# Sample attention: the matmuls of a four-page unit as one group on TensorE, and the next transposition directly behind the weighted sum

## The chip, the core and the metric

The kernel runs on one core of one Trainium2 chip. The metric is the device time of one launch in microseconds (us). The kernel before was timed three times: 3252.61, 3260.63 and 3261.89 us, median 3260.63 us. One further execution was recorded by the hardware profiler, and every duration below is from that record.

The engines in the tables are PE (TensorE, matmuls), PEld (TensorE's weight loads), DVE (VectorE), ACT (ScalarE), POOL (GpSimd) and SP (SyncE, which here only issues DMAs). Each engine works through its own instructions strictly in program order.

## What is computed

One inference step of a hybrid layer for a prompt of 2048 tokens and, with the same weights, for 8 sample tokens that each attend over 16384 cached positions. For the samples the attention works on the cached latents directly. Cut to what matters here:

```python
q_lat   = einsum('bthd,rhd->bthr', q_nope, w_uk)                  # 8 samples, 8 heads, 256 latent dims
s_past  = einsum('bthr,bkr->bhtk', q_lat, c_past) + einsum('bthd,bkd->bhtk', q_rope, kr_past)
p       = softmax(concat([s_past, s_new]) * SCALE)
o_lat   = einsum('bhtk,bkr->bthr', p[..., :P], c_past) + ...      # P = 16384 = 128 pages of 128
o       = einsum('bthr,rhd->bthd', o_lat, w_uv)
# around it, for the prompt: gated MLP, causal attention, output projection, then
up = h @ w_up;  c = causal conv of width 3 over up;  y = (silu(c_gate) * c_val) @ w_down
```

`c_past` and `kr_past` are gathered through a page table: every sample has 128 pages, scattered over a pool.

## The kernel before

**The main work.** The prompt sets the order: input projections (up to about 330 us of the profile), gated MLP (to 570), causal attention (to 1130), output projection (to 1368), and then the feed-forward part in three token blocks of 688, 688 and 680 columns. A block runs through 22 feature steps. A feature step has four quarters, Q0 to Q3 (gate and value, each in two halves of the columns). Each quarter is 24 up-projection matmuls (`up`, 8 groups of 3) whose result DVE takes out of PSUM (`U`, L1727). Behind the matmuls of Q1, Q2 and Q3 stand 5, 5 and 6 pieces of the down-projection of the step before (`dp`, 3 matmuls each, three PSUM buffers), and DVE adds each piece to the output in SBUF (`y`, L1580), in program order. Behind the pieces of Q1 and Q3 follows the convolution: ACT forms `c` from `U` (L1556), DVE adds the two other taps (two SCALAR_TENSOR_TENSOR, L1557 and L1558). The weights are split into a high and a low part ahead of use: ACT writes the high part (`wdh` behind the pieces of Q1, `wu` behind those of Q2 and of Q3), POOL the low part (`wdl`, `wu`, L124).

**The sample attention** is a second stream of work, written as a generator (`sample_stream`). After every main matmul group the helper `fill(ns)` takes the nominal time of the group off a counter; when the counter is down to zero the next piece of the stream is issued, and its `yield` value is added to the counter. So a `yield` says how much main work goes on all engines' queues before the next piece. `st["per"]` sets the pace: 27000, 24000, 28000 and 20500 ns of main work for eight pages in the four stages; a unit of four pages has half of it.

The 8 samples are handled as two sets (s = 0, 1) of four samples, and each set in two phases of 32 units. Four tiles, one for each sample, hold the four pages of a unit.

- *Scores* (first half of the generator): 36 matmuls into one PSUM tile `sc`, nine rounds (`m`) of four samples. A sample uses 32 columns of the array, so that the four matmuls of a round sit in four column strips. Each fp32 matmul stands as two records in the profile, so that a unit has 72. Between rounds 2 and 3, and between 5 and 6, stands `yield 1400`. Then DVE takes the scores out of PSUM together with a running maximum (`S`, L705), the four tiles are given back, and `pump()` issues the DMAs for the tiles that came free on SP's queue. The pool has six tiles: two of the next unit are already on their way when a unit runs, and the other two can be fetched only when it is done.
- *Weighted sum* (second half): 16 matmuls into `po` with the transposed probabilities `pT` (8 columns of the array for each sample). `pT` of the next unit is made by `turned`: a transposition on TensorE (`pp`, L767) of a 128x128 part of `S`, and a copy out of PSUM on ACT (`pT`, L85). It stands 3000 ns of main work behind the sum.

The set s = 0 is scored during gated MLP and attention (336 to 925 us) and summed during the end of the attention, the output projection and the first feature steps (1001 to about 1550). The set s = 1 is scored in feature steps 7 of the first block to 1 of the second (1577 to 2055) and summed in steps 4 to 19 of the second block (2133 to 2600).

Of the kernel before, what the change touches and what calls it, by code (L numbers as in the profile page):

```python
# [28 lines left out]
NPG = 128  # L29
# [21 lines left out]
def build(tc, A):  # L51
# [17 lines left out]
    def mkpool(stack, name, bufs, space=None):  # L69
        kw = {} if space is None else {"space": space}  # L70
        return stack.enter_context(tc.tile_pool(name=name, bufs=bufs, reuse_waits="tile", **kw))


    def mm(out, w, x, start, stop):
        pe.matmul(out, lhsT=w, rhs=x, start=start, stop=stop)  # L75
# [8 lines left out]
    def copy(out, in_):  # L84
        act.activation(out, in_, AF.Copy)  # L85
# [505 lines left out]
    st = {"wait": 0.0, "done": False, "pool": mkpool(smp, "s_pg", SL), "slots": SL, "per": PA}  # L591

    def sample_stream():
# [9 lines left out]
        def slot(shape, name):  # L603
            return st["pool"].tile(shape, F32, tag="pg", bufs=st["slots"], name=name)
# [13 lines left out]
        def load_wuv(t):  # L618
            gq.dma_start(out=t, in_=A["w_uv"].rearrange("(k p) n -> p k n", p=128))
            return t  # L620

        def load_wx():
            k = 8 - left.pop()
            wx.append(slot([128, 1024], "wos"))
            gq.dma_start(out=wx[-1], in_=A["w_out"][k * 128:(k + 1) * 128, :])
# [3 lines left out]
        def pump():  # L629
            while held["n"] < st["slots"]:  # L630
                if not pending:
                    u = plan()
                    if u is None:
                        return
                    queue.append((u, []))
                    pending.extend((u, queue[-1][1], b) for b in range(4))
                (s, kind, p0, n), got, b = pending.pop(0)
                held["n"] += 1
                bb = 4 * s + b
                _, vs = nc.values_load_multi_w_load_instructions(  # L640
                    pt[bb:bb + 1, p0:p0 + n], engines=[SPE], min_val=0, max_val=NPOOL - 1,
                    skip_runtime_bounds_check_because="the table is clamped to the pool on the chip")
                if kind == 0:
                    t = slot([128, n, 288], "ct")
                    for j in range(n):
                        sp.dma_start(out=t[:, j, :], in_=A["cT"][bass.ds(vs[j], 1), :, :].rearrange("a p f -> p (a f)"))
                else:
                    t = slot([128, n // 4, 1024], "cn")
                    for j in range(n):
                        sp.dma_start(out=t[32 * (j % 4):32 * (j % 4) + 32, j // 4, :],  # L650
                                     in_=A["cN"][bass.ds(vs[j], 1), :, :].rearrange("a p f -> p (a f)"))
                got.append(t)

        def units(s, kind):
            done = 0
            while done < NPG:
                pump()
                if not queue:
                    yield None
                    continue  # L660
                (s_, kind_, p0, n), cts = queue.pop(0)
                assert (s_, kind_) == (s, kind) and len(cts) == 4
                done += n
                yield p0, n, cts
# [14 lines left out]
        for s in range(2):  # L679
# [6 lines left out]
            for unit in units(s, 0):  # L686
                if unit is None:
                    yield None
                    continue
                p0, n, cts = unit  # L690
                N = n * 32
                ps = sps.tile([128, 512], F32, tag="sc", name="sc")
                for m in range(9):
                    for b in range(4):
                        bb = 4 * s + b
                        o = ps[32 * b:32 * b + 32, 0:N]
                        if m < 8:
                            a, q = m // 4, m % 4
                            mm(o, qz[:, b, a, q, :], cts[b][:, :, a * 128 + 32 * q:a * 128 + 32 * q + 32], m == 0, False)
                        else:  # L700
                            mm(o, qrb[:, bb, :], cts[b][:, :, 256:288], False, True)
                    if m in (2, 5):
                        yield 1400
                j += 1
                dve.tensor_scalar(out=S[:, p0 * 32:p0 * 32 + N], in0=ps[:, 0:N], scalar1=1.0, scalar2=tops[:, j - 1:j] if j else NEG,  # L705
                                  op0=ALU.mult, op1=ALU.max, accum_out=tops[:, j:j + 1])
                held["n"] -= 4
                pump()
                yield st["per"] * n / 8 - 2800
            cnew = sc_p.tile([1, 4 * KVR], F32, tag="cnew", bufs=1, name="cnew")  # L710
            gq.dma_start(out=cnew, in_=A["o_slat"][4 * s:4 * s + 4, :].rearrange("(a b) k -> a (b k)", a=1))
            ps = sps.tile([128, 512], F32, tag="sc", name="scn")
# [52 lines left out]
            def turned(p0):  # L765
                pp = sps.tile([128, 512], F32, tag="sc", name="pp")
                pe.transpose(pp[:, 0:128], S[:, p0 * 32:p0 * 32 + 128], ident)  # L767
                pT = sc_p.tile([128, 128], F32, tag="pT", name="pT")
                copy(pT, pp[:, 0:128])
                return pT  # L770

            pT = turned(0)
            yield 3000
            for unit in units(s, 1):
                if unit is None:
                    yield None
                    continue
                p0, n, cns = unit
                if s == 1 and p0 + n == NPG:
                    wuv = load_wuv(slot([128, 2, 512], "wuv"))  # L780
                    load_wx()
                for q in range(4):
                    for b in range(4):
                        mm(po[32 * b:32 * b + 8, 0:256], pT[:, 32 * b + 8 * q:32 * b + 8 * q + 8],
                           cns[b][:, 0, q * 256:(q + 1) * 256], False, p0 + 4 == NPG and q == 3)
                held["n"] -= 4
                pump()
                yield 3000
                if p0 + 4 < NPG:
                    pT = turned(p0 + 4)  # L790
                yield st["per"] / 2 - 3000
            if s == 1:
                for _ in range(4):
                    load_wx()
# [62 lines left out]
        aq.dma_start(out=x2_sp[:, SEQ:TOK].rearrange("(k p) t -> p k t", p=128), in_=a)  # L857

    stream = sample_stream()

    def step():
# [1069 lines left out]
```

## Time and profile before

| | |
|---|---|
| three runs | 3252.61, 3260.63, 3261.89 us |
| profiled execution, first to last instruction | 3243.1 us (the profile gives no other time of this execution; the runs are 9.5 to 18.8 us above it) |
| PE busy | 3071.8 us, 95% |
| DVE, ACT, POOL busy | 63%, 37%, 34% |
| mean granted TensorE clock | 0.982 of full speed |
| DMA queues | q1 (SP's) 359.85 MB, q0 (POOL's) 196.59 MB |

The page lists, for each group of instructions, the busy time, the mean of one, and the idle time of the engine just before them with what ended it. PE is the engine to watch. A matmul is pipelined: its record is longer than the distance to the next one, so costs on PE are read from start to start, not from the records' lengths. The view by line merges both rounds and stages; the view of waits can be cut to a stretch of time, which tells the stages apart.

### The profile page before, as it was taken

To read this page: it belongs to the slowest core of one execution; us is meant where nothing else is said; L and a number is where in the kernel's file an instruction comes from. 1 tells how busy PE (TensorE), PEld (TensorE's weight loads), DVE (VectorE), ACT (ScalarE), POOL (GpSimd) and SP (SyncE) were. 2 spreads that over 40 slices of the span, in tenths; PEclk is the share of its full clock that TensorE was granted. 3 is DMA by queue.
4 is the path that set the end of the run, shared out by engine and by line. 5 is a ranking of instruction groups with operands and counts; after the bars stand their busy time and mean duration, and the time that the engine had idled before them with its cause. 6 is when DMAs were issued, how large, how long until landed. Compare 5 with 4: busy or idle time off the path is not lost. (4 is left out here: it accounts for less than half of the span.)

```text
span 3243.1 us, 66014 instructions
## 1 busy us (share of the span) xinstructions
PE 3071.8 (95%) x23958; PEld 2712.4 (84%) x23958; DVE 2038.9 (63%) x3670; ACT 1193.1 (37%) x2472; POOL 1098.3 (34%) x1102
## 2 busy tenths in 40 slices
PE   7999999999999999999999999999998998999997
PEld 7898777777777788889988898889887878989987
DVE  6555332676777744445666666766566668777777
ACT  5334332676787722232222223422222233322223
POOL 4332222422233244433332234433222334333332
PEclk9999999899999999999999999999999999999999
DMA  5446667777766789987566777658766634221222
GB/s 171 131 156 225 194 194 199 202 207 199 208 162 155 198 246 251 250 238 218 179 213 206 215 218 225 200 146 216 205 190 182 188 126 143 66 72 59 66 72 53
DMA packets 340434, 571.22 MB, mean 176 GB/s; under 512 B 59343, under 2 KB 247406, under 8 KB 340110
## 3 DMA queue, kind: packets, MB, share of 16 engines
q1 hardware_dynamic: 264128, 359.85, 38.6%
q0 software_dynamic: 56176, 196.59, 20.8%
q10 hardware_dynamic: 19806, 10.55, 1.1%
q8 instruction: 192, 3.15, 0.4%
q14 instruction: 132, 1.08, 0.1%
HBM read 504.62 MB, written 62.18 MB: 175 GB/s over the span
## 5 line engine op out<-in xcount | busy, mean ns | idle before, releaser
L75 PE MATMUL up<-h,wu 128*128 128x344 f32 (+2 forms) x6336 | 1068.9, 324 | 9.5 <-DVE U L1727 4.1
L75 PEld LDWEIGHTS up<-h,wu 128*128 128x128 f32 x6336 | 1002.2, 190 | 48.7 <-issue 29.8
L1580 DVE TENSOR_TENSOR y<-y,dp 128x344 f32<-128x344 f32 (+1 forms) x960 | 456.8, 510 | 49.4 <-PE dp L75 40.1
L124 POOL TENSOR_TENSOR wu<-wraw,wu 128x1024 fp32r<-128x1024 f32 x132 | 317.9, 2409 | 363.0 <-ACT wu L85 186.8
L124 POOL TENSOR_TENSOR wdl<-wraw,wdh 128x1024 fp32r<-128x1024 f32 x66 | 158.1, 2395 | 722.8 <-ACT U L1555 683.0
L75 PE MATMUL dp<-gh,wdh 128*128 128x344 f32 (+1 forms) x960 | 323.4, 337 | 78.7 <-DVE y L1580 78.6
L1556 ACT ACTIVATE c<-U,gn 128x688 f32<-128x688 f32 (+3 forms) x138 | 128.9, 934 | 653.1 <-DVE U L1727 653.1
L1727 DVE TENSOR_TENSOR U<-up,R 128x344 f32<-128x344 f32 (+2 forms) x264 | 134.5, 511 | 351.2 <-PE up L75 344.5
L75 PE MATMUL dp<-gl,wdh 128*128 128x344 f32 (+1 forms) x960 | 310.0, 323 | 0.0
L75 PE MATMUL dp<-gh,wdl 128*128 128x344 f32 (+1 forms) x960 | 309.4, 322 | 0.0
L75 PEld LDWEIGHTS dp<-gh,wdh 128*128 128x128 f32 x960 | 182.0, 190 | 106.6 <-DVE y L1580 94.4
L75 PE MATMUL s<-k,q 96*128 96x512 f32 (+2 forms) x960 | 259.0, 381 | 4.4 <-DVE mx L1201 2.1
L1557 DVE SCALAR_TENSOR_TENSOR c<-U,gn,c 128x688 f32<-128x688 f32 (+3 forms) x138 | 214.7, 1556 | 33.4 <-ACT c L1556 33.3
L124 DVE TENSOR_TENSOR pl<-t,ph 128x512 fp32r<-128x512 f32 (+1 forms) x320 | 194.2, 607 | 63.7 <-ACT ph L85 60.7
L1558 DVE SCALAR_TENSOR_TENSOR c<-U,gn,c 128x688 f32<-128x688 f32 (+3 forms) x138 | 223.7, 1621 | 4.9
L85 ACT ACTIVATE ph<-t 128x512 fp32r<-128x512 f32 (+1 forms) x320 | 170.1, 532 | 138.2 <-PE t L1223 134.2
L1211 ACT ACTIVATE S<-S,nm 128x512 f32<-128x512 f32 (+2 forms) x320 | 208.0, 650 | 6.8 <-POOL nm L1203 6.8
L75 PEld LDWEIGHTS s<-k,q 96*128 96x128 f32 x960 | 169.7, 193 | 46.7 <-issue 9.4
L75 PEld LDWEIGHTS dp<-gl,wdh 128*128 128x128 f32 x960 | 183.2, 191 | 1.2
L75 PEld LDWEIGHTS dp<-gh,wdl 128*128 128x128 f32 x960 | 182.6, 190 | 0.9
L1223 PE MATMUL t<-cst,S 128*128 128x128 f32 x1088 | 174.9, 275 | 2.4 <-DVE pl L124 2.1
L75 PE MATMUL sc<-ct,qz 128*32 128x128 f32 x4096 | 157.5, 279 | 13.1 <-DMA ct<-in_cT 13.1
(377 smaller groups left out, 5094.7 us busy)
## 6 DMA issues: line engine op xcount, KB each, us to landing
ct<-in_cT SPq DMA_DIRECT2D x1024, 144.0 KB
cn<-in_cN SPq DMA_DIRECT2D x1024, 128.0 KB
wraw<-in_w_up POOLq DMA_DIRECT2D x132, 512.0 KB, 4.1
wraw<-in_w_down POOLq DMA_DIRECT2D x66, 512.0 KB, 4.5
q_sp<-qs SPq DMA_DIRECT2D x48, 256.0 KB
xt<-in_xT SPq DMA_DIRECT2D x16, 512.0 KB
kn_sp<-qs SPq DMA_DIRECT2D x32, 256.0 KB
v_sp<-v SPq DMA_DIRECT2D x16, 512.0 KB
```

What stands on the lines that cost most here:

```text
L75: pe.matmul(out, lhsT=w, rhs=x, start=start, stop=stop)
L85: act.activation(out, in_, AF.Copy)
L124: (lo_eng or dve).tensor_sub(lo, src, f(hi))
L1211: act.activation(s, s, AF.Exp, scale=SCALE, bias=d["nm"][:, qb:qb + 1], accum_out=d["ls"][:, qb, r:r + 1])
L1223: pe.transpose(p[:, (qb - q0) * 128:(qb - q0) * 128 + 128], d["S"][qb, kb // 4][:, ks], ident)
L1556: act.activation(c[:, lo:hi], u[:, 2 + lo:2 + hi], AF.Identity, scale=w[2], bias=g(B_CONV, ix))
L1557: dve.scalar_tensor_tensor(out=c[:, lo:hp], in0=u[:, 1 + lo:1 + hp], scalar=w[1], in1=c[:, lo:hp], op0=ALU.mult, op1=ALU.add)
L1558: dve.scalar_tensor_tensor(out=c[:, lo:hp], in0=u[:, lo:hp], scalar=w[0], in1=c[:, lo:hp], op0=ALU.mult, op1=ALU.add)
L1580: dve.tensor_add(y, y, p[:, 0:nn])
L1727: dve.tensor_mul(u[:, 2 + o:2 + o + m], p[:, 0:m], RT[b][:, o:o + m])
```

## The change

The two inner `yield 1400` of the scores go, and the `yield` behind a unit grows by the same 2800 ns. The transposition for the next unit moves from 3000 ns of main work behind the weighted sum to directly behind it, ahead of the return of the tiles. The numbers of matmuls, transpositions, copies and DMAs stay the same, and so does the distance from the start of one unit to the start of the next in main work.

```diff
                             mm(o, qrb[:, bb, :], cts[b][:, :, 256:288], False, True)
-                    if m in (2, 5):
-                        yield 1400
                 j += 1
                 dve.tensor_scalar(out=S[:, p0 * 32:p0 * 32 + N], ...)
                 held["n"] -= 4
                 pump()
-                yield st["per"] * n / 8 - 2800
+                yield st["per"] * n / 8
...
+                if p0 + 4 < NPG:
+                    pT = turned(p0 + 4)
                 held["n"] -= 4
                 pump()
-                yield 3000
-                if p0 + 4 < NPG:
-                    pT = turned(p0 + 4)
-                yield st["per"] / 2 - 3000
+                yield st["per"] / 2
```

The order of PE's instructions at three places, the rows before with a minus and the changed ones with a plus. First, a unit of scores in the feed-forward part, in step 9 of the first block, among the pieces `dp` of Q2. `x12` is a group of 12 matmuls (24 records), `qrb` the last round.

```order
 L75 MATMUL dp<-gl,wdh 128x344
 L75 MATMUL dp<-gh,wdl 128x344
-L75 MATMUL sc<-ct,qz 32x128 x12
+L75 MATMUL sc<-ct,qz 32x128 x32
+L75 MATMUL sc<-ct,qrb 32x128 x4
 L75 MATMUL dp<-gh,wdh 128x344
 L75 MATMUL dp<-gl,wdh 128x344
```

All 36 now stand where the first 12 stood; the second and third group leave their places further on, in the `up` matmuls of Q3. All 64 units are changed in this way. DVE's `S` comes directly behind the group, so that it too stands earlier: here behind the second `y` of Q2.

Second, the weighted sum of s = 0 in step 2 of the first block: `po` stands among the five pieces of Q1, `pp` stood in the `up` matmuls of Q2.

```order
 L75 MATMUL dp<-gh,wdl 128x344
 L75 MATMUL po<-cn,pT 8x256 x16
+L765 MATMUL pp<-cst,S 128x128
 L75 MATMUL dp<-gh,wdh 128x344
 L75 MATMUL dp<-gl,wdh 128x344
...
 L75 MATMUL up<-h_5_18550,wu 128x344
-L767 MATMUL pp<-cst,S 128x128
 L75 MATMUL up<-h_6_18554,wu 128x344
 L75 MATMUL up<-h_6_18555,wu 128x344
```

The transposition moves from the `up` matmuls of Q2 in among the pieces of Q1 or right behind them. This is so in steps 1 to 5 of the first block. On ACT its copy `pT` comes ahead of `wdh` and of `c` of Q1 both before and now.

Third, the weighted sum of s = 1 in step 11 of the second block: `po` stands in the `up` matmuls of Q1, `pp` stood behind the five pieces of Q1.

```order
 L75 MATMUL po<-cn,pT 8x256 x16
+L765 MATMUL pp<-cst,S 128x128
 L75 MATMUL up<-h_6_27338,wu 128x344
 L75 MATMUL up<-h_6_27339,wu 128x344
...
 L75 MATMUL dp<-gl,wdh 128x344
 L75 MATMUL dp<-gh,wdl 128x344
-L767 MATMUL pp<-cst,S 128x128
 L75 MATMUL up<-h_0_27094,wu 128x344
 L75 MATMUL up<-h_0_27095,wu 128x344
```

Here the transposition moves out of the neighbourhood of the pieces, up into the `up` matmuls of Q1. In steps 11 to 19 of the second block it stood behind three, four or all five pieces of Q1; in steps 4 to 10 it stood in the `up` matmuls of Q2 and now goes into the `up` matmuls of Q1 or right behind them (in step 4 behind the first piece). The second transposition of each step, which stands in Q3, stays in Q3.

## The prediction

> **What bounds the kernel now.** I read the page first, then the waits of TensorE cut by stage, then the order of time around single units. The page:
>
> ```profile
> span 3243.1 us, 66014 instructions
> PE 3071.8 (95%) x23958; PEld 2712.4 (84%) x23958; DVE 2038.9 (63%) x3670; ACT 1193.1 (37%) x2472; POOL 1098.3 (34%) x1102
> ...
> L75 PE MATMUL sc<-ct,qz 128*32 128x128 f32 x4096 | 157.5, 279 | 13.1 <-DMA ct<-in_cT 13.1
> ```
>
> TensorE is busy for 95% of the span. 4096 records in 157.5 us of busy time are 38 ns each: four column strips overlap. The stretches in which the units run, by busy time of each engine (PE, PEld, DVE, ACT, POOL), then the granted clock, DMA share and GB/s:
>
> ```profile
> 575.00:925.00 350.00, 340.40 (x3062) 269.21 (x3062) 251.83 (x672) 237.64 (x608) 97.51 (x212) 0.98 0.77 206
> 1583.00:2055.00 472.00, 450.54 (x4464) 406.78 (x4463) 311.42 (x480) 123.05 (x207) 157.77 (x117) 1.00 0.71 216
> 2133.00:2600.00 467.00, 440.26 (x3338) 393.60 (x3338) 283.55 (x408) 109.98 (x205) 146.20 (x102) 0.97 0.70 195
> ```
>
> These are scoring in attention, scoring in the feed-forward part, and the weighted sum of s = 1. What TensorE waits for: first in 575 to 925, then in 1583 to 2055 (two rows), then in 2133 to 2600:
>
> ```profile
> PE sc L75 <- DMA ct<-in_cT: 6.4, 5, 3.1
> ...
> PE dp L75 <- DVE y L1580: 13.5, 12, 1.6
> PE sc L75 <- DMA ct<-in_cT: 6.7, 4, 3.9
> ...
> PE dp L75 <- DVE y L1580: 26.7, 9, 3.4
> ```
>
> In attention TensorE hardly waits for DVE or ACT, so time saved on TensorE there is time of the span. In the feed-forward part it waits for `y`: a fourth piece `dp` needs the buffer that DVE's first `y` frees. These waits have causes that the change moves, so they are terms of the sum.
>
> **Term 1, entries and exits of TensorE.** One unit of scores in the gated MLP, TensorE alone:
>
> ```profile
> 476.65 0.40 PE L75 MATMUL pu<-wa,hl 128*128 128x512 f32 x1
> 476.98 0.86 PE L75 MATMUL sc<-ct,qz 128*32 128x128 f32 x24
> 477.77 0.73 PE L75 MATMUL pu<-wa,hh 128*128 128x512 f32 x2
> 478.34 0.40 PE L75 MATMUL pu<-wa,hl 128*128 128x512 f32 x1
> 478.57 0.63 PE L75 MATMUL pu<-wa,hh 128*128 128x512 f32 x2
> 479.04 0.40 PE L75 MATMUL pu<-wa,hl 128*128 128x512 f32 x1
> ...
> 481.76 0.64 PE L75 MATMUL sc<-ct,qz 128*32 128x128 f32 x16
> 482.22 0.40 PE L75 MATMUL sc<-ct,qrb 128*32 128x128 f32 x8
> 482.55 0.73 PE L75 MATMUL pu<-wa,hh 128*128 128x512 f32 x2
> ...
> 477.33 0.51 PE L75 MATMUL sc<-ct,qz 128*32 128x128 f32 x12
> ```
>
> From `pu hl` to `pu hl` with a group between: 478.34 - 476.65 = 1.69 us; without: 479.04 - 478.34 = 0.70. A visit of 24 records costs 0.99 us. Inside, 16 records take 482.22 - 481.76 = 0.46 us, and 12 (the first 12 of the row that starts at 476.98, up to 477.33) take 0.35: four more records cost 0.11. Six such rounds are 0.66, so 0.33 us of each visit is neither matmul nor main work. A unit has three visits and keeps one: 2 x 0.33 x 64 units = 42 us. The bound below: if only the stretch from the first `sc` to the next `pu` (0.79 us) were shared, 0.79 - 0.66 = 0.13 is saved, 17 us in all. I take 42, since entry, exit and the late second `pu` are each tied to a change between the two kinds of matmul, and two of three changes go.
>
> The transposition gets no price. Its 64 instances occupy little, and whether one costs more or less behind `po` than alone this trace does not show:
>
> ```profile
> L767 PE MATMUL pp<-cst,S 128*128 128x128 f32 x64 | 17.5, 273 | 0.0
> ```
>
> Both ends lie within a fraction of 17.5 us; I take 0 with 4 either way.
>
> **Term 2, waits for pages.** The tiles are given back behind the first 36 matmuls instead of 2800 ns of main work later, and the next unit starts as far from this one as before. So a page has 2.8 us more. The waits are 6.4 + 6.7 = 13.1 us; the two longest (3.1, 3.9) would leave 0.3 and 1.1: 12 us saved. Below: 5, if SP's queue is itself late. POOL's queue issues as before.
>
> **Term 3, waits for `y` while scoring.** One step (DVE, ACT, POOL and TensorE mixed), with no transposition in it:
>
> ```profile
> 1628.02 0.52 DVE L1727 TENSOR_TENSOR U<-up,R 128x344 f32<-128x344 f32 x1 [0.67 <-PE up L75]
> ...
> 1630.72 2.39 POOL L124 TENSOR_TENSOR wu<-wraw,wu 128x1024 fp32r<-128x1024 f32 x1 [4.81 <-ACT wu L85]
> 1630.83 3.02 DVE L1557 SCALAR_TENSOR_TENSOR c<-U,gn,c 128x688 f32<-128x688 f32 x1
> ...
> 1633.88 3.24 DVE L1558 SCALAR_TENSOR_TENSOR c<-U,gn,c 128x688 f32<-128x688 f32 x1
> 1633.98 2.40 POOL L124 TENSOR_TENSOR wu<-wraw,wu 128x1024 fp32r<-128x1024 f32 x1
> ...
> 1637.47 2.32 DVE L1580 TENSOR_TENSOR y<-y,dp 128x344 f32<-128x344 f32 x5
> 1638.02 0.43 PE L75 MATMUL dp<-gh,wdh 128*128 128x344 f32 x1 [1.49 <-DVE y L1580]
> ```
>
> Both DVE passes of the convolution run beside a pass of POOL and take 3.0 and 3.2 us, and `y` comes late. TensorE waited 1.49 us although one visit (0.99) stood ahead of the fourth piece: uncovered it would be 2.5. In steps 8 to 20 the whole group now stands ahead of the fourth piece, with 0.33 + 18 x 0.11 = 2.3 us of cover, 1.3 more. Most of the 13.5 us goes. In half of the steps the group stands ahead of the first piece, and DVE takes `S` before `y`, which hands back some 0.4. I take 9 saved, ends 0 and 13.
>
> **Term 4, the transposition in the feed-forward part.** On ACT the copy `pT` is ahead of `wdh` and `c` of its quarter; they wait for TensorE to reach `pp`. Step 11 of the second block, where `pp` stood behind the pieces of Q1, and step 2 of the first block, where it stood in Q2:
>
> ```profile
> 2332.24 0.27 PE L767 MATMUL pp<-cst,S 128*128 128x128 f32 x1
> 2332.72 1.05 ACT L85 ACTIVATE wdh<-wraw 128x1024 fp32r<-128x1024 f32 x1
> 2333.76 0.95 ACT L1556 ACTIVATE c<-U,gn 128x688 f32<-128x688 f32 x1
> 2334.75 2.23 DVE L1557 SCALAR_TENSOR_TENSOR c<-U,gn,c 128x688 f32<-128x688 f32 x1 [1.79 <-ACT c L1556]
> 2337.02 3.22 DVE L1558 SCALAR_TENSOR_TENSOR c<-U,gn,c 128x688 f32<-128x688 f32 x1
> 2341.14 0.42 PE L75 MATMUL dp<-gh,wdh 128*128 128x344 f32 x1 [3.43 <-DVE y L1580]
> ...
> 2342.20 3.43 PE L75 MATMUL up<-h,wu 128*128 128x344 f32 x12
> ...
> 2347.52 2.15 PE L75 MATMUL up<-h,wu 128*128 128x344 f32 x12
> ...
> 1434.75 2.07 PE L75 MATMUL po<-cn,pT 128*8 128x256 f32 x32
> 1437.97 0.93 DVE L1557 SCALAR_TENSOR_TENSOR c<-U,gn,c 128x688 f32<-128x688 f32 x1
> 1438.93 0.94 DVE L1558 SCALAR_TENSOR_TENSOR c<-U,gn,c 128x688 f32<-128x688 f32 x1
> 1440.17 0.27 PE L767 MATMUL pp<-cst,S 128*128 128x128 f32 x1
> ```
>
> In the first case `c` follows `pp` by 1.5 us, DVE's passes start 1.79 us late, collide with POOL, and TensorE waits 3.43. In the second the passes take 0.93 and 0.94 and nobody waits. The change exchanges the cases.
>
> - *Second block, steps 11 to 19*: `pp` leaves the pieces. The nine waits, 26.7 us, go, and so does the slow clock behind them (twelve records took 3.43 us instead of 2.15, at most 1.3 x 9 = 12): 27 + 10. Something returns in all sixteen steps 4 to 19, because no `pp` stands in Q2 any more and POOL's `wu` of that quarter runs beside DVE's passes. One such collision costs 3.0 - 0.93 = 2.1 us, against the 2.5 for two in term 3: 0.5 remains. In steps 4 to 7 `po` and `pp` stand right ahead of the pieces or among them and hold `wdh` and `c` too: about 1.5. 4 x 1.5 + 12 x 0.5 = 12 lost.
> - *First block, steps 1 to 5*: `pp` comes among or behind the pieces of Q1, as in the first case. 26.7 / 9 = 3.0 a step, 15 us of new waits, and 5 x 1.2 = 6 for the clock: 21 lost.
>
> The Trainium skill speaks against this part ("TensorE: Matmul & The Clock Gate", section "What's actually happening"): an idle window of about 3.4 us takes TensorE to half its clock for as long again. The rows of 2341 and 2342 agree. By the rule most of the five new waits of 3.0 would not fill such a window, and the sum would be some 6 us lower; if each did, 1.7 apiece, 2 us higher.
>
> **Term 5, given back in attention.** A unit is one long interruption instead of three, and the main work between is uninterrupted for 12000 ns instead of 9200. DVE has 251.83 us of work in 350 us there, of which the visits, 20 x 2.97 = 59 us, leave 291 of main work: 87% on DVE, 82% on ACT. TensorE stays the bound, with little room in two PSUM buffers; I give back 4 us, bounds 0 and the 13 that 20 units gain there.
>
> **The sum.** -42 - 12 - 9 - 37 + 12 + 21 + 4 = -63 us. The profiled span is 3243.1 us, so the span afterwards would be 3180. The runs lie 9.5 to 18.8 us above the span. What lies around it does not change, so I take the same difference from the median: 3260.6 - 63 = 3198 us.
>
> **The rivals.**
>
> *Absorbed (chance 0.17).* DVE and ACT run out of room in attention, and in the feed-forward part the shorter step only lengthens the waits for `y`. For it: 87% of DVE. Against: no wait of TensorE for `S` or `ph` stands among the larger rows of 575 to 925. Then the 13 us of attention and the 9 of term 3 are not gained: 3198 + 13 - 4 + 9 = 3216.
>
> *The copy costs at every place (0.09).* In the first block it stands among the pieces of Q3 too; if both quarters cost 3.0 + 1.2, ten times, 42 are lost instead of 21, and in the second block the collisions with POOL return in full (16 x 2.5 = 40 instead of 12): 3198 + 21 + 28 = 3247. Against it: before, `pp` stood among the pieces of Q3 in most of steps 4 to 18, and no wait beyond the nine is listed.
>
> *Slower: DVE held by the scores (0.04).* `S` waits for all 36 matmuls, and behind it in DVE's order stand `y` and the passes of the convolution. If in each of the 32 units of 1577 to 2055 the whole 2.3 us reaches TensorE as a wait, that is 74 us and term 3 is lost as well: 3198 + 9 + 74 = 3281. The other terms gain 63 - 9 = 54, so it decides from 54 / 32 = 1.7 us a unit. Against it: TensorE's own `dp` come behind the same group, so that the hold mostly coincides with it.
>
> **How the numbers follow.** My forecast has 0.70. Its own range is 3180 to 3216: terms 1 and 2 at their lower bounds (25 + 7) do not go together with the worst of term 4. With the rivals at 3216 and partly 3247, a range of 3177 to 3232 leaves out about 2 in 10. A measurement of this kernel tells 0.3%, 9.8 us, from no change: faster is below 3250.8. Faster has the forecast, "absorbed" and half of the third case, 0.92; the same has 0.05; slower has 0.03.
>
> **What would show it.** Right: in the order of time one `sc` row of 72 records per unit, 2.3 us from its neighbour to its neighbour; waits for `ct` near 1 us; no wait for `y` above 1.5 us in steps 11 to 19 of the second block, and new ones of about 3 us in steps 1 to 5 of the first, with the clock below 1.00 in 1400 to 1550. Wrong: a visit of 72 records that takes near 2.97 us; new rows of TensorE waiting for `S`, `ph` or `pl` in attention; waits for `y` spread over all steps of the feed-forward part.

## The result

The changed kernel takes 3178.2 us (median of four runs, 3174.17 to 3179.65), the kernel before 3256.6 us (four runs, 3252.14 to 3261.89): a ratio of 0.9767, 95% interval 0.975 to 0.9784, or 78 us less. The forecast was 3198 us with a range of 3177 to 3232; the time lies 1 us inside the range's lower end, and below the 3180 to 3216 that the forecast had as its own. The head of the page after:

```profile
span 3177.2 us, 66010 instructions
PE 3028.7 (95%) x23958; PEld 2725.0 (86%) x23958; DVE 2043.0 (64%) x3670; ACT 1196.2 (38%) x2472; POOL 1097.9 (35%) x1102
```

Between the two profiled executions the span falls by 3243.1 - 3177.2 = 65.9 us, against 63 in the sum. TensorE's busy time falls by 43.1 us, the other 23 are idle time. A unit of scores in the gated MLP, TensorE alone (start, duration, engine, line, operation, tiles, kinds, count):

```profile
362.75 0.40 PE L75 MATMUL pu<-wa,hl 128*128 128x512 f32 x1
363.08 1.95 PE L75 MATMUL sc<-ct,qz 128*32 128x128 f32 x64
364.85 0.40 PE L75 MATMUL sc<-ct,qrb 128*32 128x128 f32 x8
365.18 0.73 PE L75 MATMUL pu<-wa,hh 128*128 128x512 f32 x2
365.75 0.39 PE L75 MATMUL pu<-wa,hl 128*128 128x512 f32 x1
366.44 0.40 PE L75 MATMUL pu<-wa,hl 128*128 128x512 f32 x1
```

One visit of 72 records: 365.75 - 362.75 - (366.44 - 365.75) = 2.31 us, where three visits took 3 x 0.99 = 2.97. That is 0.66 us for each of 64 units, 42 us.

What TensorE waits for, cut to 1010 to 1400 (first two rows), 1400 to 1583, 1583 to 2055 and 2133 to 2600 (source, total, count, longest):

```profile
PE po L75 <- DMA cn<-in_cN: 8.9, 4, 4.5
...
PE dp L75 <- DVE y L1577: 3.4, 1, 3.4
...
PE dp L75 <- DVE y L1577: 11.3, 4, 3.0
...
PE dp L75 <- DVE y L1577: 5.8, 10, 2.8
...
PE dp L75 <- DVE y L1577: 7.3, 12, 1.1
```

No row of these stretches, nor of 575 to 925, names the pages `ct` any more; before they stood for 13.1 us. In the first block five new waits have come, 3.4 + 11.3 us; while scoring in the feed-forward part the waits for `y` fell from 13.5 to 5.8, and in the second block from 26.7 to 7.3. The changed kernel is earlier in its work at the same time, so these stretches don't hold quite the same steps. Counted by steps, the waits while scoring (steps 8 to 20) fell from 13.5 to 3.0 us, and the 2.8 in the row stands in step 1 of the second block, behind the last unit; in steps 4 to 19 of the second block they fell from 26.7 to 8.8, with one of 1.6 in step 4 and none over 0.7 in steps 11 to 19. The stretches as wholes (busy time of PE, PEld, DVE, ACT, POOL, then clock, DMA share, GB/s):

```profile
1400.00:1583.00 183.00, 171.66 (x1319) 157.56 (x1319) 112.45 (x166) 43.50 (x80) 57.38 (x39) 0.96 0.66 181
...
2133.00:2600.00 467.00, 457.90 (x3413) 403.71 (x3413) 288.40 (x447) 121.58 (x223) 158.66 (x114) 1.00 0.74 196
```

The slow clock has moved with the long waits: it was 0.97 in 2133 to 2600 and is 1.00 now, and it is 0.96 in 1400 to 1583, where it was 1.00. Step 2 of the first block, all engines in order of time:

```profile
1417.84 0.33 PE L765 MATMUL pp<-cst,S 128*128 128x128 f32 x1
...
1418.20 0.28 ACT L85 ACTIVATE pT<-pp 128x128 f32<-128x128 f32 x1 [6.36 <-PE pp L765]
...
1418.38 1.05 ACT L85 ACTIVATE wdh<-wraw 128x1024 fp32r<-128x1024 f32 x1
...
1419.42 0.95 ACT L1553 ACTIVATE c<-U,gn 128x688 f32<-128x688 f32 x1
1419.51 2.40 POOL L124 TENSOR_TENSOR wdl<-wraw,wdh 128x1024 fp32r<-128x1024 f32 x1 [10.30 <-ACT U L1552]
...
1420.40 2.25 DVE L1554 SCALAR_TENSOR_TENSOR c<-U,gn,c 128x688 f32<-128x688 f32 x1 [1.20 <-ACT c L1553]
...
1422.68 3.22 DVE L1555 SCALAR_TENSOR_TENSOR c<-U,gn,c 128x688 f32<-128x688 f32 x1
...
1422.79 2.38 POOL L124 TENSOR_TENSOR wu<-wraw,wu 128x1024 fp32r<-128x1024 f32 x1
...
1426.81 0.65 PE L75 MATMUL dp<-gh,wdh 128*128 128x344 f32 x1 [2.95 <-DVE y L1577]
...
1427.26 0.49 PE L75 MATMUL dp<-gl,wdh 128*128 128x344 f32 x1
...
1427.55 0.49 PE L75 MATMUL dp<-gh,wdl 128*128 128x344 f32 x1
```

Read it downwards: the copy `pT` has held ACT for 6.36 us, until `pp` was done, and only then do `wdh` and `c` come. DVE's two passes, which took 0.93 and 0.94 us here before, start late and run beside POOL's passes, which wait for the same ACT instructions: 2.25 and 3.22. The fourth piece of Q2 waits 2.95 us for `y`. Behind the wait the matmuls start 0.29 us apart, at half of the usual pace.

### The profile page after: what moved, and what is told of

Read it like the earlier page. It is cut to its first block, busy times and chain, and to the rows that moved or that the text cites. A ratio compares the mean times of both kernels' runs of the same rounds, so it can differ in the third digit from the quotient of the medians.

```text
span 3177.2 us, 66010 instructions
## 1 busy us (share of the span) xinstructions
PE 3028.7 (95%) x23958; PEld 2725.0 (86%) x23958; DVE 2043.0 (64%) x3670; ACT 1196.2 (38%) x2472; POOL 1097.9 (35%) x1102
## 5 line engine op out<-in xcount | busy, mean ns | idle before, releaser
L75 PE MATMUL up<-h,wu 128*128 128x344 f32 (+2 forms) x6336 | 1052.0, 322 | 12.0 <-DVE U L1724 4.5
L1555 DVE SCALAR_TENSOR_TENSOR c<-U,gn,c 128x688 f32<-128x688 f32 (+3 forms) x138 | 236.8, 1716 | 4.9
L1554 DVE SCALAR_TENSOR_TENSOR c<-U,gn,c 128x688 f32<-128x688 f32 (+3 forms) x138 | 212.8, 1542 | 23.8 <-ACT c L1553 23.8
L85 ACT ACTIVATE wu<-wraw 128x1024 fp32r<-128x1024 f32 x132 | 138.3, 1050 | 67.3 <-DMA wraw<-in_w_up 62.5
```

What stands on the lines that cost most here:

```text
L1554: dve.scalar_tensor_tensor(out=c[:, lo:hp], in0=u[:, 1 + lo:1 + hp], scalar=w[1], in1=c[:, lo:hp], op0=ALU.mult, op1=ALU.add)
L1555: dve.scalar_tensor_tensor(out=c[:, lo:hp], in0=u[:, lo:hp], scalar=w[0], in1=c[:, lo:hp], op0=ALU.mult, op1=ALU.add)
```

## The experiments

Kernels that ran together are compared with runs of the kernel before on the same chip; ratios are to these (median 3255.6 us for the first four, 3248.1 for the next four). The changed kernel's 0.9767 is to a median of 3256.6, so for the next four a difference in microseconds to the changed kernel comes out some 5 us lower than by the two ratios; both are given.

### The scores alone

```diff
-                    if m in (2, 5):
-                        yield 1400
...
-                yield st["per"] * n / 8 - 2800
+                yield st["per"] * n / 8
```

(in the kernel before; the transposition stays)

> The kernel before with the first part of the change alone: a unit of scores is one group of 36 matmuls (72 records), its tiles are given back behind it, and the transposition stays 3000 ns of main work behind the sum. My theory (the parts are additive): entries and exits -42 us, the waits for pages -13, the waits for y in 1583 to 2055 from 13.5 to about 4 (-9), 4 back in attention. The weighted sums stay as they were: no waits for y in steps 1 to 5 of the first block, nine of about 3 us in steps 11 to 19 of the second. Together about -60 us against the kernel before: span near 3183, ratio near 0.981. Rival (most of the gain came with the transposition, and the price of an entry is paid by waits elsewhere): less than 25 us faster, ratio above 0.992.

3189.7 us, ratio 0.9791 (0.9764 to 0.9818): 66 us less. Its waits for `y` in 1400 to 1583 and 2133 to 2600:

```profile
PE dp L75 <- DVE y L1578: 0.4, 1, 0.4
...
PE dp L75 <- DVE y L1578: 26.8, 9, 3.4
```

The nine waits of the second block are untouched, and the first block has no long one. So nearly all of the gain, five sixths, is the scores', and what they do is independent of the transposition. The rival of a gain from the transposition falls.

### The transposition alone

```diff
+                if p0 + 4 < NPG:
+                    pT = turned(p0 + 4)
                 held["n"] -= 4
                 pump()
-                yield 3000
-                if p0 + 4 < NPG:
-                    pT = turned(p0 + 4)
-                yield st["per"] / 2 - 3000
+                yield st["per"] / 2
```

(in the kernel before; the scores stay in three groups)

> The kernel before with the second part of the change alone: the next transposition directly behind the sum, the scores in three groups. My theory: five new waits for y of about 3 us with slow clock behind them in 1400 to 1583 (+21 to +23), the nine waits of the second block gone (26.7 us to below 10, -25 to -28): between -7 and 0 us against the kernel before, ratio 0.998 to 1.000, and the three groups of the scores as dear as before. Rival (the waits of the first block come from the scores being one group, not from the transposition): no new waits in 1400 to 1583, and -25 us, ratio 0.992.

3242.6 us, ratio 0.9956 (0.994 to 0.9973): 13 us less, where I expected 0 to 7. Between the two profiles the span falls by 3243.1 - 3241.0 = 2.1 us, as expected (the further profiles of the kernel before, below, tell where the rest comes from). The same two rows:

```profile
PE dp L75 <- DVE y L1579: 14.8, 5, 3.4
...
PE dp L75 <- DVE y L1579: 11.0, 14, 2.2
```

The five new waits come without any change of the scores, so they are the transposition's. (The 2.2 us stand in step 3 of the second block and stood there before, outside the stretch.) The two parts add: 66 + 13 = 79 us against 78 for both.

### Each set by itself

```diff
-                if p0 + 4 < NPG:
-                    pT = turned(p0 + 4)
                 held["n"] -= 4
                 pump()
-                yield st["per"] / 2
+                gap = 0 if s else 3000
+                yield gap
+                if p0 + 4 < NPG:
+                    pT = turned(p0 + 4)
+                yield st["per"] / 2 - gap
```

(in the changed kernel; in the second run `gap = 5000 if s else 3000`)

> The changed kernel, with the transposition back 3000 ns of main work behind the sum for s = 0 and directly behind it for s = 1. My theory: the waits for y in steps 1 to 5 of the first block (3.42, 2.95, 2.96, 2.95 and 2.48 us in the changed kernel) fall to below 0.5 each and the half clock behind them goes, which is 21 to 23 us; the second block stays as in the changed kernel (7.3 us of waits, none above 1.2). About 22 us less than the changed kernel: span near 3155, ratio to the kernel before near 0.970. Rival (the long waits there have another cause, such as the units of scores being one block): no change against the changed kernel, ratio 0.977.

3159.9 us, ratio 0.9705 (0.9677 to 0.9733): 18 us below the changed kernel, or 20 by the two ratios; the first block's loss stood at 21 in the sum.

```profile
PE dp L75 <- DVE y L1579: 0.4, 1, 0.4
...
PE dp L75 <- DVE y L1579: 6.2, 11, 1.1
```

The waits of the first block are gone. This kernel differs from the one with the scores alone only by the place for s = 1, and is 3189.7 - 3159.9 = 30 us faster: that is the worth of the second block's part (25 in the sum).

> The changed kernel with the transposition 3000 ns of main work behind the sum for s = 0 and 5000 ns behind it for s = 1, so that in the second block it stands in the quarter Q2 in most steps. My theory: as with s = 0 alone put back, and in the second block ACT holds wdh and both wu behind the copy until DVE's passes are through, so that POOL does not run beside them: the waits of 7.3 us in 2133 to 2600 fall to about 2. Span near 3150, ratio 0.968. Rival (the place 5000 falls among the pieces of Q1 in some steps): new waits of about 3 us there, 9 to 27 us more, ratio 0.971 to 0.977.

3145.6 us, ratio 0.9653 (0.9625 to 0.968): the fastest of all, 33 us below the changed kernel. In steps 4 to 19 of the second block no wait for `y` of a piece is listed. Step 13 of that block, DVE, ACT and POOL around the transposition, and the stretch as a whole:

```profile
2327.54 0.93 DVE L1556 SCALAR_TENSOR_TENSOR c<-U,gn,c 128x688 f32<-128x688 f32 x1
2328.50 0.94 DVE L1557 SCALAR_TENSOR_TENSOR c<-U,gn,c 128x688 f32<-128x688 f32 x1
...
2329.10 0.28 ACT L85 ACTIVATE pT<-pp 128x128 f32<-128x128 f32 x1 [2.70 <-PE pp L765]
2329.27 2.00 ACT L85 ACTIVATE wu<-wraw 128x1024 fp32r<-128x1024 f32 x2
2330.41 2.40 POOL L124 TENSOR_TENSOR wu<-wraw,wu 128x1024 fp32r<-128x1024 f32 x1 [6.81 <-ACT wu L85]
```

```profile
2090.00:2560.00 470.00, 470.00 (x3535) 417.55 (x3533) 267.86 (x460) 122.32 (x226) 162.26 (x116) 1.00 0.76 203
```

The copy holds ACT here too, 2.70 us, but now between the convolution and `wu`: POOL gets its pass only when DVE is through, both of DVE's passes take 0.93 us, and TensorE is busy for 470.00 of 470 us. A hold on ACT hurts or helps by what stands behind it.

### Two groups and nine groups

```diff
                             mm(o, qrb[:, bb, :], cts[b][:, :, 256:288], False, True)
+                    if m == 4:
+                        yield 1400
...
-                yield st["per"] * n / 8
+                yield st["per"] * n / 8 - 1400
```

(in the changed kernel; for nine groups `if m < 8: yield 350`, and `- 2800` behind the unit)

> The changed kernel with the scores of a unit in two groups (40 and 32 records) with 1400 ns of main work between them, the tiles given back behind the second. My theory (each group pays for its entry and exit, 0.33 us): 64 x 0.33 = 21 us more than the changed kernel, near 3199 us, ratio to the kernel before near 0.982. Rival (what pays is the early release of the tiles or the uninterrupted main work behind a unit): the pages still come in time, and no more than 5 us are lost; ratio 0.978 or less.

3203.1 us, ratio 0.9855 (0.9826 to 0.9884): 25 us above the changed kernel, or 29 by the two ratios; the price of an entry and exit explains 21, the rest is of the size of its few waits for pages (2.3 us) and more wait for `y` (8.4 us in steps 8 to 20, against 3.0).

> The changed kernel with the scores of a unit in nine groups of one round of four column strips (8 records), 350 ns of main work between them. My theory: eight more entries and exits per unit, 8 x 0.33 x 64 = 169 us more than the changed kernel, near 3347 us. A visit of 8 records should take 0.33 + 2 x 0.11 = 0.55 us. Rival (the price belongs to long groups, such as the first matmul behind them that finds its weights late): a short visit costs less than 0.4 us and the whole less than 90 us more.

3303.6 us in its only run, 125 above the changed kernel (131 by the two ratios), less than the 169 expected. A visit of 8 records among the pieces:

```profile
1725.06 0.32 PE L75 MATMUL dp<-gl,wdh 128*128 128x344 f32 x1
1725.22 0.32 PE L75 MATMUL dp<-gh,wdl 128*128 128x344 f32 x1
1725.47 0.43 PE L75 MATMUL sc<-ct,qz 128*32 128x128 f32 x8
1725.82 0.42 PE L75 MATMUL dp<-gh,wdh 128*128 128x344 f32 x1
1726.08 0.32 PE L75 MATMUL dp<-gl,wdh 128*128 128x344 f32 x1
```

From the piece's last matmul ahead (1725.22) to the second one behind (1726.08) are 0.86 us; two usual distances of 0.16 off, the visit costs 0.54. The price was as expected, the number of groups was not: 350 ns is less than some main groups take in the count, rounds adjoined, and the trace has 407 groups (253 of 8 records, 139 of 16, 15 of 24) instead of 576. 407 - 64 = 343 more visits at 0.33 us are 113 of the 125 us. Over the visits that stand between matmuls of the feed-forward part, the medians give 0.32 or 0.33 us for visits of 8, 16, 24, 32, 40 and 72 records.

### Tiles given back later

```diff
+                yield 2800
                 held["n"] -= 4
                 pump()
-                yield st["per"] * n / 8
+                yield st["per"] * n / 8 - 2800
```

(in the changed kernel, behind a unit of scores)

> The changed kernel, but the tiles of a unit's pages are given back 2800 ns of main work behind its group, as late as in the kernel before; the group stays whole. My theory: TensorE's waits for pages come back, up to 13.1 us in 575 to 925 and 1583 to 2055, so 8 to 15 us more than the changed kernel, ratio to the kernel before 0.979 to 0.981. Rival (the waits went because the whole unit starts where the third group stood, or they come and go between executions): no waits for pages above 2 us, ratio 0.977.

3187.1 us, ratio 0.9812 (0.9781 to 0.9842), 9 us above the changed kernel's median, or 15 by the two ratios, where 8 to 15 were expected; the two intervals just touch. The waits for pages in 1583 to 2055 are back, as long as before (6.7):

```profile
PE sc L75 <- DMA ct<-in_cT: 6.5, 4, 2.2
```

In 575 to 925, where they were 6.4 us, none is listed. There the early return is not what ended them. With the scores in three groups or nine they stand there (5.0 us in the run with the transposition alone, 5.5 with nine groups), with one or two groups they are at most 1.2; why, no run tells. So the reason that I gave for term 2, the earlier return, is shown for the feed-forward part alone.

### The copy later, the transposition not

```diff
-                    pT = turned(p0 + 4)
+                    pp = turned(p0 + 4)
...
-                yield st["per"] / 2
+                yield 3000
+                if p0 + 4 < NPG:
+                    pT = copied(pp)
+                yield st["per"] / 2 - 3000
```

(in the changed kernel; `turned` leaves out the copy, `copied` is the copy alone)

> The changed kernel with the transposition directly behind the sum on TensorE, but ACT's copy of it 3000 ns of main work later, for both s. My theory (the order on ACT is the cause: the copy holds wdh, c and wu behind it): in steps 1 to 5 of the first block the waits of 14.8 us fall below 2 and the half clock goes (-20), while in the second block neither wu is held any more where the copy stood, so that POOL collides with both DVE passes in more steps: 7.3 us of waits become 10 to 30. Between -20 and +5 us against the changed kernel, ratio 0.971 to 0.978, with the waits of the first block below 2. Rival (the place of the transposition on TensorE is the cause): the waits in 1400 to 1583 stay at 11 us and more, ratio 0.977.

3155.7 us, ratio 0.9712 (0.968 to 0.9744): 22 us below the changed kernel, or 18 by the two ratios. Waits for `y` in 1400 to 1583 and 2133 to 2600:

```profile
PE dp L75 <- DVE y L1583: 2.9, 2, 2.5
...
PE dp L75 <- DVE y L1583: 2.6, 8, 0.7
```

`pp` stands on TensorE where the change put it, and still four of the five long waits are gone. The cause is the order on ACT; the transposition's place on TensorE by itself costs nothing that can be seen. Two points of my expectation missed. One wait of 2.5 us stays, in step 5, where both DVE passes run beside POOL (3.05 and 3.23 us). And in the second block I expected 10 to 30 us of collisions and found 2.6 us of waits: in steps 4 to 7 the second pass takes 0.94 us and nobody waits, and from step 8 on POOL meets only one of the two passes, which costs TensorE 0.7 us or less.

### The kernel before, twice more

> The kernel before itself, profiled once more. Its profile on record has a span of 3243.1 us, its other executions spans of 3237 to 3266 with a median near 3252, so that the change's 66 us between the two profiles on record and its 78 us between the medians differ by 12. My theory: the profiled execution was a quick one, in which the waits for pages of the weighted sum (6.2 us) and the half clock behind the nine waits were small; another shows the same nine waits of 26.7 us, with more half clock (up to 1.3 us for each wait of 3) or more waits for DMA: 5 to 20 us more in span, all of it in those rows. Rival (the time around the program differs): the same span of 3243 and a run 10 us or more above it.

> As the look before: the same rows for y, and a span between 3237 and 3266 us whose excess over 3243.1 stands in waits for DMA and in stretches of half clock.

Spans 3255.3 and 3252.7 us, times 3257.07 and 3254.51. So what lies around the span is 1.8 us, as in the changed kernel (3178.97 with a span of 3177.2). The rival is out: the profiled execution of the prediction was itself 10 to 12 us quicker than these. The waits for `y` in 2133 to 2620 are the old ones, 26.8 us in the first of them and in the second:

```profile
PE dp L75 <- DVE y L1580: 26.7, 9, 3.4
```

What differs is behind and between them. From the start of the same instructions on DVE, the second falls back by 6.8 us from 1010 to 1414 us (the waits for the tiles of the weighted sum grew from 6.2 to 10.6 us, and the clock went from 0.98 to 0.97) and by 6.5 us from 2121 to 2626 (the stretches of the second, clock third from the end; 2133 to 2600 was at 0.97):

```profile
1010.00:1400.00 390.00, 364.10 (x2921) 315.21 (x2922) 204.16 (x390) 160.79 (x366) 143.77 (x203) 0.97 0.87 232
2133.00:2600.00 467.00, 440.86 (x3301) 395.40 (x3299) 285.39 (x410) 110.60 (x207) 140.38 (x95) 0.96 0.70 190
```

Half clock followed eight of the nine waits in either execution, and six in the execution of the prediction. The traces hold the granted clock as a list of stretches: in steps 4 to 19 of the second block it stood at half for 37.5 us in either, against 23.9 in the execution of the prediction. Half of that is lost, 18.8 against 12.0, and the difference of 6.8 is what the second block lost (6.5, and 6.6 in the first of the two, which lost 6.0 in the other stretch).

## Why the prediction was right, term by term

| term | predicted | shown by |
|---|---|---|
| 1, entries and exits | -42 | visit of 72 records 2.31 us instead of 2.97: -42; 0.33 us again in two and nine groups |
| 2, pages | -12 | 13.1 us of waits gone; a late return brings 6.5 back in the feed-forward part, none in attention |
| 3, `y` while scoring | -9 | 13.5 to 3.0 in steps 8 to 20: -10.5 |
| 4, second block | -25 | -27 between the two profiles, -30 between the medians of two kernels that differ in this alone |
| 4, first block | +21 | +23 between the profiles (waits of 14.8 us, and half of 17.1 us at half clock), 18 by putting s = 0 back |
| 5, given back in attention | +4 | 3.5, but not in attention |
| sum | -63 | -65.9 in span |

The profile rows come from the start of the same DVE instruction (the second `U` of a feature step) in both: it moved from 1388.9 to 1364.9 in step 0 of the first block (-24.0), from 1541.3 to 1540.0 in step 6 (-1.3), from 2036.6 to 2001.3 in step 0 of the second block (-35.3), from 2139.1 to 2099.7 in step 4 (-39.4) and from 2610.4 to 2543.5 in step 20 (-66.9). Up to the first block 32 units at 0.66 and the 6.4 us of pages, 27.5 us, should have been gained; 24.0 were, so 3.5 were given back. That this is the size of term 5 is luck, since attention gave back little or nothing: from its first `s` (574.8 and 569.4) to the first `op` (1134.0 and 1108.8) it fell from 559.2 to 539.4, and 20 units at 0.66 with the 6.4 us of pages make 19.6. (The kernel before has one stretch of half clock there, 758.7 to 762.1, that the changed one lacks; at most its 1.7 us can have been given back.) Of the 3.5 us, 1.8 stand ahead of the first `pu` (305.1 and 306.9), before any unit, 0.7 in the gated MLP, and 1.2 behind the first `op`. The transposition's price of 0 held: `po` and `pp` together take 2.10 us in place of 2.04 and 0.11 apart.

**What failed is the step from the span to the time**: "What lies around it does not change, so I take the same difference from the median." I took the 9.5 to 18.8 us between the profile's span and the runs for time around the program. It is 1.8 us, and the rest is the spread of the span: other executions of the kernel before have more half clock and longer waits for DMA. The forecast of 3198 is 20 us above the measured time: 12 from the quick execution, 4 because the median of the kernel before is 3256.6 with a fourth run (it was 3260.6 with three), 3 from the sum and 1 from the changed kernel's own profile. Of the 78.4 us between the medians 65.9 are between the two profiles, 11.7 are the quick execution before (3256.6 against 3243.1 + 1.8), and 0.7 the changed kernel's own (3179.0 against 3178.2). The change removes the nine waits behind which half clock comes in some executions and not in others, so it should also have been costed with more than the six that this one execution showed: term 4 gave 10 us to the clock, where this execution lost 12 and the two others 19. By these two the second block's part is worth some 6 us more than between the two profiles. The remaining 5 us of the quick execution stand in the stretch of 1010 to 1414 us; which part of them the change could touch, the runs don't tell.

The return of the cost in the second block (12 predicted) came out at 8.8 us of waits, 4.8 in steps 4 to 7 and 4.0 in steps 8 to 19, for which 6 and 6 were taken; it is the same term, sized a little too high.

**The rivals.** "Absorbed": TensorE's row for `sc` shows no new wait, 575 to 925 has TensorE busy for 348.83 of 350 us (340.40 before), attention is 19.8 us shorter, and the scores alone bring 66 us. "The copy costs at every place" asked for waits in Q3 of the first block and full collisions in the second: neither is there. "DVE held by the scores" asked for waits of 1.7 us and more in 32 units of 1577 to 2055: those in steps 8 to 20 sum to 3.0 us, none over 0.5.

**The clock.** The Trainium skill ("TensorE: Matmul & The Clock Gate", section "What's actually happening") gives the half-clock state to TensorE after at least one idle window of about 3.4 us, by which most of the five new waits would have kept the full clock. The measurement decides against that reading here: four of the five, 2.48 to 3.42 us long, were followed by half clock. The Trainium skill adds that the window runs freely, which agrees with a wait of 2.96 us that has the full clock behind it while one of 2.95, a step earlier, has half.

The traces tell these two apart. The granted clock changes in them only on a grid of 3.41 us from one possible change to the next. The windows of that grid, two for the wait of 2.95 us, then three for the wait of 2.96 (length, busy time of PE, PEld, DVE, ACT, POOL, then clock, DMA share, GB/s):

```profile
1422.95:1426.36 3.41, 0.91 (x6) 0.62 (x4) 3.41 (x3) 0.00 (x0) 2.78 (x2) 1.00 0.91 249
1426.37:1429.78 3.41, 2.97 (x10) 2.97 (x11) 2.26 (x5) 0.00 (x0) 0.00 (x0) 0.50 1.04 226
...
1453.68:1457.09 3.41, 1.76 (x12) 1.47 (x10) 3.38 (x2) 0.00 (x0) 2.97 (x3) 1.00 0.92 263
1457.10:1460.50 3.40, 2.10 (x13) 2.11 (x14) 3.07 (x7) 0.00 (x0) 0.51 (x1) 1.00 1.08 258
1460.51:1463.92 3.41, 3.41 (x24) 3.41 (x23) 0.50 (x2) 0.00 (x0) 0.00 (x0) 1.00 0.82 219
```

The first wait leaves one window idle for 2.50 us, and the next window has half clock. The second is split into 1.65 and 1.30, and no window has half clock.

## What to carry to other kernels

Count the changes between small-tile and full-tile matmuls on TensorE, not only the matmuls: here each round trip cost 0.33 us whatever stood between, and one group in place of three saved 42 us over 64 units. When an instruction moves, follow what its consumer holds back on another in-order engine; the best place for the transposition was not early or late, but where the copy's wait held back only what should be held. Before the difference to a measured median is taken for overhead, look at several executions: waits that bring the clock down on some executions make a single profile too quick or too slow.

## What I had not expected of the hardware

- It is enough that a part of one window of 3.41 us is idle to bring TensorE to half its clock. Over the twelve traces 78 waits for `y` are 2.0 to 3.5 us long. Each of the 65 that took 1.91 us or more out of one window was followed by half clock, and none of the 13 that took 1.89 us or less. Where the wait falls on the grid thus decides: half clock followed 54 of the 65 waits of 2.4 to 3.5 us, and only one of 166 waits of 1.3 to 1.7 us. In other stages some windows with 1.2 to 1.9 us of idle time were followed by half clock too; what decides there, the runs don't tell.
- Behind the same waits at the same places the clock differs between executions, because the grid lies differently: six, eight and eight of nine in three profiles of one kernel. Its 13 runs on one chip spread over 3247 to 3268 us; four runs there of the kernel without these waits (3000 and 5000 ns) stay within 3140 to 3149.
